# Attention in a fused trunk kernel: probability transposes in groups of two tiles, value products one group behind, across query blocks

## The chip, the core and the metric

The kernel runs on one core of a Trainium2 chip. The metric is the device time of one execution in microseconds. Five engines work from queues of their own, each in order: TensorE (PE for its matrix products, PEld for its weight loads), VectorE (DVE), ScalarE (ACT), GpSimd (POOL) and SyncE (SP), which here issues all DMA transfers.

## The reference, cut to what matters

One layer of a decoder: RMS norm, an input projection, then a diagonal state-space mixer (SSM with a gated unit, GLU) beside a causal attention with forget gates, an output projection, and a squared-ReLU MLP. The part that the change touches is the attention, in float32, with 8 heads of 64 over 2048 positions:

```python
s = einsum('bhqd,bhkd->bhqk', qb, kb) * scale
s = s + csum[:, :, q0:kend, None] - csum[:, :, None, :kend]
s = where(mask, s, -inf)
p = softmax(s, axis=-1)
out = einsum('bhqk,bhkd->bhqd', p, vb)
```

## The kernel before, in words

Full float32 products are made of three (in attention two) products of reduced-precision operands: each operand is split into a rounded part (`h`) and a remainder (`l`).

Attention goes head by head (`h`, 8 of them), and within a head over 8 blocks `b` of 256 queries, each of two rows of 128. For a block, `s_units` makes the scores: for each row and each 512 keys two matmuls into a PSUM bank `s` (L796, L797), of which there are three, then DVE adds the mask and keeps a running minimum (L800), and ACT takes the exponential of the row (L804), into a buffer `p`.

`t_units` then works over `j`, one step for 256 keys. `tr(j)` transposes the four 128x128 tiles of `p` on PE into one PSUM bank `t`, of three (L832; the three tiles on the diagonal in L839 to L841). ACT copies the bank to the rounded part `th` (L853), and DVE makes the remainder `tl` from bank and `th` (L854). `th` and `tl` have THB = 3 buffers each; the diagonal uses `lasth` and `lastl`, two of each. `pv(j)` multiplies `vs` with them: L863 with `th` and L864 with `tl`, twice each, all adding up in the one PSUM bank `o` of the block. A list of steps holds the order: transposes of `j`, then products of `j-1`:

```python
hold[j] = tr(j)
if j:
    pv(j - 1, hold.pop(j - 1))
```

The products of the last `j` close the block, `fin1` copies `o` to `ot` (L868), and `fin2`, put off until after the next block's steps, transposes `ot` back (L874), adds its halves (L877, L878) and stores them to `o_d` (L879).

Between blocks a generator (`side`) issues pieces of the SSM (L587 to L643) and the GLU (L699 to L725), whose matmuls run on the same PE. When the attention's pools are closed, the output projection takes their memory: `woh` and `wol` are made on ACT (L979) and DVE (L980) from loaded weights, and L1019 to L1021 multiply with them. So `woh` waits until the last `oo` is stored.

What is written is not yet the order on the engines. A scheduler places all instructions, engine by engine, by the order in which they are written and by its own estimate of when their operands are ready; so instructions of neighbouring blocks and of the side work stand between the steps above.

Of the kernel before, what the change touches and what calls it, by code (L numbers as in the profile page):

```python
# [37 lines left out]
AHEAD = 1  # L38
LAG = 3
TAB = 2  # L40
THB = 3
SPRI = 150
FGJ = 5
FGC = 3
# [23 lines left out]
def f32(ap):  # L68
    return ap.bitcast(F32)


def body(tc, a, out, stop=None):
# [3 lines left out]
    with ctx:  # L76
# [657 lines left out]
        with ExitStack() as pb:  # L734
# [20 lines left out]
            def load_head(h):  # L755
                r0 = h * HD
                k2 = k2s[h % 2]
                k1 = kv[h % 2].tile([P, L], R, tag="k1", name="k1") if h else AT["k1"]
                vs = (kv1v if h % 2 else kv0).tile([P, NT, P], R, tag="vs", name="vs") if h else AT["vs"]
                nc.sync.dma_start(out=f32(k1[0:HD]), in_=kh_d[r0:r0 + HD])  # L760
                nc.sync.dma_start(out=f32(k1[HD:]), in_=kh_d[r0:r0 + HD])
                nc.sync.dma_start(out=f32(k2[0:HD]), in_=kl_d[r0:r0 + HD])
                nc.sync.dma_start(out=f32(k2[HD:HD + 2]), in_=c_d[h])
                nc.sync.dma_start(out=f32(vs), in_=v_d[h])
                hd[h] = (k1, k2, vs)
# [56 lines left out]
            def t_units(h, b):  # L822
                po = {}

                def tr(j):
                    q0, q1 = pt_[h, 2 * b], pt_[h, 2 * b + 1]
                    pt = ps_t.tile([P, CH], F32, tag="t", name="t")
                    if j < b:
                        k = 0
                        for kt in (2 * j, 2 * j + 1):  # L830
                            for q in (q0, q1):
                                T.transpose(pt[:, k:k + P], q[:, kt * P:(kt + 1) * P], ident)  # L832
                                k += P
                        th = ab.tile([P, CH], R, tag="th", name="th", bufs=THB)
                        tl = ab.tile([P, CH], R, tag="tl", name="tl", bufs=THB)
                        o = 0
                        kts = (2 * j, 2 * j + 1)
                    else:
                        T.transpose(pt[:, 2 * P:3 * P], q0[:, 2 * j * P:(2 * j + 1) * P], ident)  # L839
                        T.transpose(pt[:, 3 * P:4 * P], q1[:, 2 * j * P:(2 * j + 1) * P], ident)  # L840
                        T.transpose(pt[:, P:2 * P], q1[:, (2 * j + 1) * P:(2 * j + 2) * P], ident)  # L841
                        th, tl = lh[nlast[0] % 2], ll[nlast[0] % 2]
                        nlast[0] += 1
                        o = P
                        kts = (2 * j + 1, 2 * j)
                    nt[0] += 1
                    if j < b and nt[0] % POOLT == 0:
                        t = ab.tile([P, CH], F32, tag="tf", name="tf")
                        S.activation(t, pt, AF.Copy)
                        G.tensor_copy(th, t)  # L850
                        G.tensor_tensor(out=tl, in0=t, in1=f32(th), op=ALU.subtract)
                    else:
                        S.activation(th[:, o:], pt[:, o:], AF.Copy)  # L853
                        V.tensor_tensor(out=tl[:, o:], in0=pt[:, o:], in1=f32(th[:, o:]), op=ALU.subtract)  # L854
                    return th, tl, kts

                def pv(j, x):
                    th, tl, kts = x
                    vs = hd[h][2]
                    if j == 0:  # L860
                        po["o"] = ps_o.tile([P, 256], F32, tag="o", name="o")
                    for n, kt in enumerate(kts):
                        T.matmul(po["o"], vs[:, kt, :], th[:, n * 256:n * 256 + 256], start=(j == 0 and n == 0), stop=False)  # L863
                        T.matmul(po["o"], vs[:, kt, :], tl[:, n * 256:n * 256 + 256], start=False, stop=(j == b and n == 1))  # L864

                def fin1():
                    ot = ab.tile([P, 256], F32, tag="ot", name="ot")
                    S.activation(ot, po["o"], AF.Copy)  # L868
                    po["ot"] = ot

                def fin2():
                    pt = ps_t.tile([P, CH], F32, tag="t", name="tt")
                    for n in range(2):
                        T.transpose(pt[:, n * P:(n + 1) * P], po["ot"][:, n * P:(n + 1) * P], ident)  # L874
                    oo = ab.tile([P, 2, HD], F32, tag="oo", name="oo", bufs=3)
                    p3 = pt[:, :256].rearrange("p (n d) -> p n d", d=P)
                    S.activation(oo, p3[:, :, HD:], AF.Copy)  # L877
                    V.tensor_tensor(out=oo, in0=p3[:, :, :HD], in1=oo, op=ALU.add)  # L878
                    nc.sync.dma_start(out=o_d[b * 256:(b + 1) * 256, h * HD:(h + 1) * HD].rearrange("(n p) d -> p n d", p=P), in_=oo)  # L879

                hold = {}
                us = []
                for j in range(b + 1):
                    def u(j=j):
                        hold[j] = tr(j)
                        if j:
                            pv(j - 1, hold.pop(j - 1))
                    us.append(u)

                def end():  # L890
                    pv(b, hold.pop(b))
                    fin1()
                us.append(end)
                return us, fin2

            load_head(0)
            defer = []
            pss = ExitStack()

            def stages():  # L900
# [9 lines left out]
            for h in range(H):  # L910
                for n, b in enumerate(FIRST if h == 0 else range(8)):
                    if n == (2 if h == 0 else 0) and h + 1 < H:
                        load_head(h + 1)
                    with tc.high_priority(offset=SPRI if h == 0 and n < 2 else 0):
                        for u in s_units(h, b):
                            u()
                    tu, fin2 = t_units(h, b)
                    for u in tu:
                        u()
                    if defer:  # L920
                        defer.pop()()
                    defer.append(fin2)
                    marks.append(next(x for x in reversed(nc.cur_bb.bb.instructions) if x.engine == mybir.EngineType.PE))
                    credit += (b + 2) * (RATE2 if wr else RATE)
                    while credit >= 1 and chunks[0] < 1:
                        credit -= 1
                        if len(marks) > LAG:
                            with tc.issue_after(marks[-1 - LAG]):
                                next(side, None)
                        else:  # L930
                            next(side, None)
            defer.pop()()
            while chunks[0] < 1:
                next(side)
# [473 lines left out]
```

## Time and profile before

| | before |
|---|---|
| median of 3 runs | 2467.52 us (2463.4 to 2474.23) |
| profiled execution | 2465.18 us, of which its span 2463.4 us |
| PE busy, share of the span | 2395.5 us, 97% |
| PE weight loads busy | 2012.4 us, 82% |
| DVE busy | 1603.4 us, 65% |
| ACT busy | 1142.8 us, 46% |
| POOL busy | 855.4 us, 35% |
| mean granted TensorE clock | 0.99 |

Attention begins with its first transposes at 407.8 us and its last value product starts at 932.9 us. "Busy" of PE counts each matmul from start to a modelled end, so neighbours overlap: the distance from one start to the next is what a matmul costs. A clock of 1.00 is 2.4 GHz, one of 0.50 is 1.2 GHz. In the groups of rows below, the "idle before" of a group is the time in which its engine did nothing, and the name behind the arrow is what ended it.

### The profile page before, as it was taken

To read this page: it belongs to the slowest core of one execution; us is meant where nothing else is said; L and a number is where in the kernel's file an instruction comes from. 1 tells how busy PE (TensorE), PEld (TensorE's weight loads), DVE (VectorE), ACT (ScalarE), POOL (GpSimd) and SP (SyncE) were. 2 spreads that over 40 slices of the span, in tenths; PEclk is the share of its full clock that TensorE was granted. 3 is DMA by queue.
4 is the path that set the end of the run, shared out by engine and by line. 5 is a ranking of instruction groups with operands and counts; after the bars stand their busy time and mean duration, and the time that the engine had idled before them with its cause. 6 is when DMAs were issued, how large, how long until landed. Compare 5 with 4: busy or idle time off the path is not lost.

```text
span 2463.4 us, 35859 instructions
## 1 busy us (share of the span) xinstructions
PE 2395.5 (97%) x12208; PEld 2012.4 (82%) x12208; DVE 1603.4 (65%) x2996; ACT 1142.8 (46%) x1914; POOL 855.4 (35%) x810
## 2 busy tenths in 40 slices
PE   7999999999999998999899999999999999999998
PEld 6988888899889877888678887788888888788886
DVE  7513424888888798767456657856775565686675
ACT  4312214777667685333344444444544444444343
POOL 2077302445443165322445443320124444332110
PEclk9999999999999999999899999999999999999999
DMA  5455534455454355666444447777764444586774
GB/s 198 133 151 163 170 120 125 112 130 129 118 127 122 75 142 160 212 227 222 143 145 149 143 160 282 246 234 239 252 203 144 137 146 154 209 290 216 247 236 148
DMA packets 286871, 428.49 MB, mean 174 GB/s; under 512 B 80656, under 2 KB 130320, under 8 KB 284112
## 3 DMA queue, kind: packets, MB, share of 16 engines
q1 hardware_dynamic: 286688, 426.21, 54.8%
q8 instruction: 96, 1.57, 0.3%
q14 instruction: 87, 0.71, 0.1%
HBM read 284.93 MB, written 141.16 MB: 173 GB/s over the span
## 4 chain that ended last, share of the span: by engine, by line
PE 56%; DVE 2%; DMA 1%; issue 1%; POOL 1%; ACT 0%; SPq 0%; DVEq 0%; ACTq 0%; POOLq 0%
PE pp L1143 8%; PE pp L1144 8%; PE pp L1145 8%; PE pp L1241 8%; PE pp L1242 8%; PE pp L1240 7%; PE po L1020 2%; PE po L1019 2%; PE po L1021 2%; PE pt L958 1%; DVE y L1106 0%; DVE olo L1233 0%; DVE olo L1099 0%; PE pz L710 0%; PE pz L709 0%
## 5 line engine op out<-in xcount | busy, mean ns | idle before, releaser
L1098 ACT ACTIVATE ohi<-raw 128x1024 fp32r<-128x1024 f32 x224 | 222.9, 999 | 432.8 <-PE pp L1144 199.8
L1099 DVE TENSOR_TENSOR olo<-raw,ohi 128x1024 fp32r<-128x1024 f32 x224 | 283.4, 1277 | 178.6 <-ACT ohi L1098 174.6
L1241 PE MATMUL pp<-olo,ohi 128*128 128x512 f32 x896 | 350.6, 391 | 3.2 <-DVE olo L1233 3.2
L1242 PE MATMUL pp<-ohi,olo 128*128 128x512 f32 x896 | 348.9, 390 | 0.0
L1240 PE MATMUL pp<-ohi 128*128 128x512 f32 x896 | 340.3, 391 | 0.7 <-ACT ohi L1232 0.7
L1143 PE MATMUL pp<-xh_t,ohi 128*128 128x512 f32 x512 | 203.1, 397 | 3.5 <-DVE u L1106 2.5
L1144 PE MATMUL pp<-xl_t,ohi 128*128 128x512 f32 x512 | 202.2, 395 | 0.0
L1145 PE MATMUL pp<-xh_t,olo 128*128 128x512 f32 x512 | 201.9, 395 | 0.0
L1241 PEld LDWEIGHTS pp<-olo,ohi 128*128 128x128 f32 x896 | 168.5, 188 | 39.0 <-DVE olo L1233 4.4
L1240 PEld LDWEIGHTS pp<-ohi 128*128 128x128 f32 x896 | 168.3, 188 | 36.5 <-ACT ohi L1232 1.3
L1242 PEld LDWEIGHTS pp<-ohi,olo 128*128 128x128 f32 x896 | 168.6, 188 | 34.8
L854 DVE TENSOR_TENSOR tl<-t,th 128x512 fp32r<-128x512 f32 x224 | 150.3, 686 | 42.3 <-ACT th L853 41.4
L804 ACT ACTIVATE p<-p,m 128x1920 f32<-128x1920 f32 (+15 forms) x128 | 154.0, 1204 | 28.4 <-DVE m L800 27.9
L1103 POOL TENSOR_TENSOR s<-h,h 128x512 f32<-128x512 f32 x32 | 57.2, 1789 | 300.1 <-DVE olo L1099 224.1
L1143 PE MATMUL pp<-xh_b,ohi 128*128 128x512 f32 x384 | 153.0, 398 | 4.4 <-DVE xl_t L961 2.4
L853 ACT ACTIVATE th<-t 128x512 fp32r<-128x512 f32 x224 | 129.0, 596 | 58.6 <-PE t L832 50.5
L1144 PE MATMUL pp<-xl_b,ohi 128*128 128x512 f32 x384 | 152.3, 397 | 0.2 <-DVE xl_b L961 0.2
L373 PE MATMUL pm<-xl,whi 128*128 128x512 f32 x384 | 152.1, 396 | 0.0
L1145 PE MATMUL pp<-xh_b,olo 128*128 128x512 f32 x384 | 152.0, 396 | 0.0
L374 PE MATMUL pm<-xh,wlo 128*128 128x512 f32 x384 | 151.8, 395 | 0.0
L372 PE MATMUL pm<-xh,whi 128*128 128x512 f32 x384 | 151.8, 396 | 0.0
L796 PE MATMUL s<-k,qs 128*128 128x512 f32 (+2 forms) x320 | 135.1, 424 | 1.5 <-DVE m L800 1.4
(438 smaller groups left out, 5975.0 us busy)
## 6 DMA issues: line engine op xcount, KB each, us to landing
raw<-q_d SPq DMA_DIRECT2D x224, 256.0 KB
raw<-in_w_down SPq DMA_DIRECT2D x224, 256.0 KB
raw<-in_w_up SPq DMA_DIRECT2D x64, 512.0 KB
q_d<-s SPq DMA_DIRECT2D x128, 256.0 KB
q_d<-h SPq DMA_DIRECT2D x96, 256.0 KB
xr<-n_d SPq DMA_DIRECT2D x48, 256.0 KB
x<-in_x SPq DMA_DIRECT2D x16, 512.0 KB
v_d<-sv SPq DMA_DIRECT2D x32, 256.0 KB
```

The costliest lines, as they stand in the source:

```text
L372: T.matmul(ps, hi[:, k, :], xh[c][:, k, :], start=(k == 0), stop=False)
L373: T.matmul(ps, hi[:, k, :], xl[c][:, k, :], start=False, stop=False)
L374: T.matmul(ps, lo[:, k, :], xh[c][:, k, :], start=False, stop=(k == KT - 1))
L804: S.activation(pr[:, :kend], pr[:, :kend], AF.Exp, bias=m[:, ch:ch + 1], scale=-1.0, accum_out=l_all[:, i, h:h + 1])
L1098: S.activation(hi[:, sl], src, AF.Copy)
L1099: V.tensor_tensor(out=lo[:, sl], in0=src, in1=f32(hi[:, sl]), op=ALU.subtract)
L1143: T.matmul(pb, wh[:, ks], XH[xn][:, k], start=start and k == 0, stop=False, skip_group_check=not start)
L1144: T.matmul(pb, wh[:, ks], XL[xn][:, k], start=False, stop=False, skip_group_check=not start)
L1145: T.matmul(pb, wl[:, ks], XH[xn][:, k], start=False, stop=stop and k == 3, skip_group_check=not start)
L1240: T.matmul(banks[i], hi[:, 0, isl], hi[:, 1], start=start and u == 0, stop=False, **sk)
L1241: T.matmul(banks[i], hi[:, 0, isl], lo[:, 1], start=False, stop=False, **sk)
L1242: T.matmul(banks[i], lo[:, 0, isl], hi[:, 1], start=False, stop=u == 15, **sk)
```

## The change: what it does

`t_units` no longer returns steps. It walks over `j` in groups of GRP = 2. For each group it first issues a `fin2` that is still put off, then the transposes of both tiles of the group (eight of them, or fewer on the diagonal), and then the value products of the group ahead of it, which lie in a list `waiting`. That list is kept across query blocks and heads: the last group of a block is multiplied only after the first group of the next block is transposed. `fin1` follows the last products of a block. `th` and `tl` get six buffers each instead of three. What an engine computes is the same, and so is the number of instructions on each engine.

```diff
-THB = 3
+THB = 6
+GRP = 2
...
-                hold = {}
-                us = []
-                for j in range(b + 1):
-                    def u(j=j):
-                        hold[j] = tr(j)
-                        if j:
-                            pv(j - 1, hold.pop(j - 1))
-                    us.append(u)
-
-                def end():
-                    pv(b, hold.pop(b))
-                    fin1()
-                us.append(end)
-                return us, fin2
+                def pvs(g):
+                    def f():
+                        for j, x in g:
+                            pv(j, x)
+                        if g[-1][0] == b:
+                            fin1()
+                            defer.append(fin2)
+                    return f
+
+                for j0 in range(0, b + 1, GRP):
+                    if defer:
+                        defer.pop()()
+                    g = [(j, tr(j)) for j in range(j0, min(j0 + GRP, b + 1))]
+                    if waiting:
+                        waiting.pop()()
+                    waiting.append(pvs(g))
...
-                    tu, fin2 = t_units(h, b)
-                    for u in tu:
-                        u()
-                    if defer:
-                        defer.pop()()
-                    defer.append(fin2)
+                    t_units(h, b)
...
+            waiting.pop()()
             defer.pop()()
```

The scheduler makes of this another order on every engine, from the first value product on. Two places of it follow. Lines of the changed kernel stand one higher in the attention (L833 for L832, L864 and L865 for L863 and L864, L875 for L874) and one lower in the output projection (L978 for L979).

The first place is on PE, in the seventh head, where a block ends and a long one begins. `t`, `th` and `tl` belong to the tiles of the new block, `lasth` and `lastl` to the diagonal of the old one. Before:

```order
L863 MATMUL o<-lasth_3761,vs 128x256
L832 MATMUL t<-ident,p 128x128 x4
L864 MATMUL o<-lastl_3763,vs 128x256
L863 MATMUL o<-lasth_3761,vs 128x256
L864 MATMUL o<-lastl_3763,vs 128x256
L832 MATMUL t<-ident,p 128x128 x8
L863 MATMUL o<-th,vs 128x256
L864 MATMUL o<-tl,vs 128x256
```

And now:

```order
L864 MATMUL o<-lasth_3761,vs 128x256
L643 MATMUL py<-abz,cs 128x256
L797 MATMUL s<-k_9382,qs 128x512
L798 MATMUL s<-k_1_3756,q_3_3459 128x512
L797 MATMUL s<-k_9382,qs 128x256
L798 MATMUL s<-k_1_3756,q_3_3459 128x256
L865 MATMUL o<-lastl_3763,vs 128x256
L864 MATMUL o<-lasth_3761,vs 128x256
L865 MATMUL o<-lastl_3763,vs 128x256
L875 MATMUL tt<-ident,ot 128x128 x2
L833 MATMUL t<-ident,p 128x128 x8
L864 MATMUL o<-th,vs 128x256
```

Before, the first `th` and `tl` of the new block come from the four transposes five rows above the products. Now those four stand ten rows further up than the piece shown, ahead of three products of the old block, four more transposes and five SSM products.

The second place is at the end of the attention. On ACT, `oo` is the last output of the attention, `woh` the first weights of the output projection, `pq` and `jk` belong to the norm of the GLU's output, and `w` and `gh` to its next chunk. Before:

```order
L877 ACTIVATE oo<-tt 128x128
L979 ACTIVATE woh_11287<-raw,gn 128x1024
L979 ACTIVATE woh_11293<-raw,gn 128x1024
L979 ACTIVATE woh_11299<-raw,gn 128x1024
L979 ACTIVATE woh_11305<-raw,gn 128x1024
```

And now:

```order
L878 ACTIVATE oo<-tt 128x128
L688 ACTIVATE w<-w 128x512 x2
L726 ACTIVATE jk,ss_s<-pq 128x512
L700 ACTIVATE gh<-gt 128x512 x2
L726 ACTIVATE jk,ss_s<-pq 128x512 x3
L978 ACTIVATE woh_11287<-raw,gn 128x1024
L978 ACTIVATE woh_11293<-raw,gn 128x1024
```

The four `jk` and their neighbours, which stood behind the first weights, now stand ahead of them. On PE the sixteen transposes that make `pq` go with them, directly behind the last two of the attention:

```order
L712 MATMUL pz<-gh,wl 128x512
L875 MATMUL tt<-ident,ot 128x128 x2
L724 MATMUL pq<-ident,sg 128x128 x16
L710 MATMUL pz<-gh,wh 128x512
L711 MATMUL pz<-gl,wh 128x512
L712 MATMUL pz<-gh,wl 128x512
```

Before, there were gate products (`pz`) there, and the transposes for `pq` came between products of the output projection.

## Rows read from the trace of the kernel before

**Rows 1.** Busy time by stage: us, PE, PEld, DVE, ACT, POOL, clock, DMA share, GB/s
```profile
407.00:934.00 527.00, 516.01 (x3536) 464.71 (x3534) 442.68 (x1095) 382.87 (x749) 233.56 (x250) 1.00 0.48 120
934.00:956.00 22.00, 15.52 (x57) 11.38 (x58) 19.06 (x26) 13.53 (x17) 11.08 (x9) 0.84 0.46 145
```

**Rows 2.** Waits of weight loads, 407 to 934 us: total us, times, longest
```profile
PEld o L864 <- DVE tl L854: 8.9, 24, 1.3
PEld s L796 <- DVE m L800: 5.1, 14, 0.7
...
PEld o L863 <- ACT ot L868: 2.5, 7, 0.6
...
PEld o L863 <- ACT th L853: 1.1, 4, 0.4
...
PEld o L864 <- DVE lastl L854: 0.4, 2, 0.2
```

**Rows 3.** Timeline around 848 us: start us, us, instruction [idle before, what ended it]
```profile
847.59 0.60 PE L832 MATMUL t<-ident,p 128*128 128x128 f32 x4
...
848.28 0.60 ACT L853 ACTIVATE th<-t 128x512 fp32r<-128x512 f32 x1 [0.38 <-PE t L832]
848.38 1.04 PE L832 MATMUL t<-ident,p 128*128 128x128 f32 x8
...
848.91 2.06 DVE L854 TENSOR_TENSOR tl<-t,th 128x512 fp32r<-128x512 f32 x3 [3.60 <-ACT th L853]
...
849.66 0.19 PEld L864 LDWEIGHTS o<-tl,vs 128*128 128x128 f32 x1 [0.26 <-DVE tl L854]
```

**Rows 4.** Timeline around 855 us, where DVE waited for a load
```profile
855.37 0.17 DVE L669 TENSOR_SCALAR gb<-gb 128x4 f32<-128x4 f32 x1 [1.46 <-DMA gb<-in_glu_b]
855.44 0.68 DVE L854 TENSOR_TENSOR tl<-t,th 128x512 fp32r<-128x512 f32 x1
...
856.18 0.19 PEld L864 LDWEIGHTS o<-tl,vs 128*128 128x128 f32 x1 [1.30 <-DVE tl L854]
```

**Rows 5.** Groups by line: xcount, busy us, mean ns, idle before, its releaser
```profile
L832 PE MATMUL t<-ident,p 128*128 128x128 f32 x896 | 130.7, 272 | 0.0
```

**Rows 6.** Timeline of PE alone around 659 us
```profile
658.60 0.60 PE L832 MATMUL t<-ident,p 128*128 128x128 f32 x4
658.95 0.36 PE L863 MATMUL o<-th,vs 128*128 128x256 f32 x1
659.15 0.28 PE L864 MATMUL o<-tl,vs 128*128 128x256 f32 x1
659.27 0.28 PE L863 MATMUL o<-th,vs 128*128 128x256 f32 x1
```

**Rows 7.** Busy time by stage at the end of attention, columns as above
```profile
932.00:938.00 6.00, 3.75 (x22) 3.09 (x21) 5.90 (x12) 2.33 (x4) 3.85 (x3) 1.00 0.50 142
938.00:944.00 6.00, 4.03 (x19) 2.81 (x18) 4.10 (x7) 1.10 (x3) 5.52 (x5) 1.00 0.05 11
944.00:950.00 6.00, 2.90 (x7) 1.62 (x8) 5.06 (x4) 6.00 (x7) 3.64 (x3) 0.76 0.29 98
950.00:956.00 6.00, 6.00 (x22) 4.73 (x21) 6.00 (x9) 5.17 (x7) 0.00 (x0) 0.67 0.88 286
```

**Rows 8.** Timeline of ACT, 939 to 961 us
```profile
939.08 0.27 ACT L877 ACTIVATE oo<-tt 128x128 f32<-128x128 f32 x1
943.75 4.27 ACT L979 ACTIVATE woh<-raw,gn 128x1024 fp32r<-128x1024 f32 x4 [4.41 <-DMA o_d<-oo]
...
950.52 1.14 ACT L687 ACTIVATE w<-w 128x512 f32<-128x512 f32 x2
...
955.63 0.57 ACT L725 ACTIVATE jk<-pq 128x512 f32<-128x512 f32 x1
956.11 0.19 ACT L725 ACTIVATION_READ_ACCUMULATOR jk<-pq 128x1 f32 x1
956.20 2.19 ACT L699 ACTIVATE gh<-gt 128x512 fp32r<-128x512 f32 x2
```

More of the change, by code (lines that the diff above doesn't have):

```diff
@@ L879, in fin2 @@
                     nc.sync.dma_start(out=o_d[b * 256:(b + 1) * 256, h * HD:(h + 1) * HD].rearrange("(n p) d -> p n d", p=P), in_=oo)
-                hold = {}
-                us = []
-                for j in range(b + 1):
-                    def u(j=j):
-                        hold[j] = tr(j)
-                        if j:
-                            pv(j - 1, hold.pop(j - 1))
-                    us.append(u)
-                def end():
-                    pv(b, hold.pop(b))
-                    fin1()
-                us.append(end)
-                return us, fin2
+                def pvs(g):
[13 more added lines that the diff above has]
+                    waiting.append(pvs(g))
             load_head(0)
-            defer = []
+            defer, waiting = [], []
             pss = ExitStack()
```

## The prediction, made before the result was known

> **What bounds the kernel now.** I read the busy time by stage first, then the waits, then the timeline at the places where they stand. By stage, the attention with its side work, from 407 to 934 us, is a stretch in which PE is busy 516 of 527 us at a clock of 1.00 [rows 1]. DVE is busy for 443 us of it and ACT for 383: neither is the bound, but DVE has little room. So a change of order can win only what PE loses in there, and PE's busy time hides some of that, since each matmul is counted to a modelled end. The waits of the weight loads show more of it [rows 2]: 8.9 us for `tl`, 0.4 for `lastl` and 1.1 for `th`, together 10.4 us in 30 waits, that is for the operands of the value products; 5.1 us for a free score bank (DVE must have read it); 2.5 us for the single bank `o`, which ACT must have emptied before the next block's first product. That is 18.0 us, or 0.7% of the time, and it is about all that the middle of the kernel can give.
>
> How such a wait comes about is seen at 848 us [rows 3]. The four transposes of a block's first tile start at 847.59 at 0.11 us apart ((1.04 - 0.27) / 7 in the eight at 848.38, 0.27 being the length of one [rows 5]), so their slot is over at 848.03. `th` starts at 848.28 and takes 0.60, the first `tl` starts at 848.91, and the weight load with it at 849.66, 1.63 us after the slot. In that time PE had three products at 0.12, eight transposes at 0.11 and one more product, 1.36 us of work. The missing 0.27 us is the wait of 0.26 that the row shows. So an undisturbed tile needs about 1.6 us of other work on PE between its transposes and its `tl`, and one more DVE instruction of 0.6 us in the way makes it 2.2 us. At 855 us it was worse: DVE sat behind a load for 1.46 us, and PE waited 1.30 us for the `tl` behind it [rows 4].
>
> At the end of attention stands the other loss: from 932 to 950 us PE is busy for 3.75, 4.03 and 2.90 of three times 6 us, idle for 7.3, and the clock then stands at 0.76 and 0.67 in two stretches [rows 7]. The chain there is the last `oo`, its store, then `woh`, since the new weights take the attention's memory: ACT idles 4.41 us until the store is done [rows 8].
>
> **The change, part by part.** No instruction is added or removed, so all of it is distance and order.
>
> *Operands of the value products.* I counted in both orders, with 0.11 us for a transpose, 0.12 for a value product, 0.23 for a score product of 512 and 0.22 for an SSM product, the PE work between the last transpose of a tile and the first product with its `tl`. Over the 288 tiles the smallest distance goes from 1.23 to 1.70 us, the median from 3.18 to 3.53, and the tiles with less than 2.2 us go from 64 to 27. At the first place shown with the change it goes from 1.36 to about 4.5 us. In proportion to those tiles, 27/64 of the 10.4 us stay, 4.4 us, and 6.0 go. But waits like that at 855 us come from DVE being held up and depend on the distance less; so I take 5.5 us of gain. The ends are 0 (all waits are of that kind) and 10.4 us.
>
> *Score banks.* There are three, and a bank is used again three score tiles later. Counted in the same way, from the end of the products of one use to the start of those of the next but two, distances under 2.0 us go from 19 to 31 of 317. In proportion the 5.1 us become 8.3, 3.2 more; most reuses are far from that limit, and the tiles in question lie only just under it, so I take a loss of 1.0 us. Ends: a gain of 5.1 (DVE, less often pressed, frees them earlier) and a loss of 3.2.
>
> *The bank `o`.* Distances under 1 us from a block's last product to the next block's first go from 13 to 10 of 63. I count nothing; the ends are a gain of 2.5 and a loss of 1.0, since ACT's queue between the two is another one now.
>
> *Alternation of transposes and products.* From transposing (or another full-precision product) to a product PE changes 346 times before and 314 times after. At 658.60 four transposes and the product behind them take 0.55 us to the start of the next but one matmul [rows 6], and 4 x 0.11 + 0.12 is 0.56: the product starts early and the one behind it later by as much. So an alternation costs nothing, and neither do 32 of them. If the 0.08 us by which the first product's slot is longer than 0.12 were all a price, it would be 2.6 us, which is the end on the gaining side.
>
> *Transpose banks.* Eight transposes need two of the three banks `t` at once. No transpose waited before (0.0 [rows 5]); the shortest twentieth of the reuse distances goes from 2.17 to 1.93 us, still over 1.6. I count nothing, with a loss of 2 us as the end, about what the `th` waits and half of the `o` waits are now. The six `th` and `tl` buffers only take away waits of ACT, which is not the bound.
>
> *The end of attention.* The sixteen transposes for `pq` now stand ahead of the output projection: 16 x 0.11 = 1.8 us of work moves into idle time. Against that, ACT no longer waits idle for the last store; it has two `w` (1.14 us), four `jk` (0.57 + 0.19 each) and two `gh` (2.19) to do between `oo` and `woh` [rows 8], 6.4 us against the 4.41 of before, so `woh` may come 2.0 us later, which is 0.2 us more than the moved work covers. The last value products themselves may be earlier, since their `lastl` has more time. I take a gain of 1.5 us; the ends are a gain of 5 (two thirds of the 7.3 us idle filled) and a loss of 6 (below).
>
> The sum: -5.5 + 1.0 + 0 + 0 + 0 - 1.5 = -6.0 us. The profiled execution took 2465.18 us, 1.8 of it outside its span; it becomes 2459 us. The median of the runs lies 2.3 us above that execution, and a rise of that size is within their own spread.
>
> **A rule that speaks against it.** In the stage of attention, with nearly 1100 transposes (896 of them in L832 [rows 5]), the clock is granted at 1.00 throughout [rows 1], the eight in a row at 848.38 included [rows 3]. The Trainium skill, in "TensorE: Matmul & The Clock Gate", Part 4 on PE-mode transpose, says that the full clock does not engage for transposes, as they don't count as PE activity in the same way. By that rule longer runs of transposes would invite falls of the clock; the trace does not agree so far, as its runs of eight did not lose it.
>
> **Rivals.**
>
> *All of the middle's waits go* (18%). All 18.0 us of rows 2 vanish and the end gives its 1.5: 2465.2 - 19.5 = 2446 us. For it: each of these waits is short (1.3 us at the longest), and the smallest distance now exceeds 1.6 us. Against it: score banks come closer together, and DVE is busy for 84% of the stage.
>
> *It does not do what it says* (24%). The scheduler fills gaps by itself and pulls the groups apart again: runs of eight transposes go from 20 to 22 only, and runs of four from 167 to 161. DVE's queue has the same work, so a product that comes later finds a `tl` that comes later, and waits move to the score banks: 2466 us, no change. For it: the median distance grew by only 0.35 us, and DVE's hold-ups [rows 4] stay.
>
> *The end of attention gets slower* (12%). The four `pq` go through one bank, so each needs its four transposes (0.44 us) and its `jk` (0.76), with the two `gh` between: 4 x 1.20 + 2.19 = 7.0 us before `woh` can start, 2.6 more than the 4.41 us. PE then idles long enough for one more fall of the clock, which cost 0.24 x 6 + 0.33 x 6 = 3.4 us of full clock in rows 7. With nothing won in the middle that is 2465.2 + 6.0 = 2471 us, slower than before. It decides if `woh` starts more than 7.3 us after `oo`, that is 2.6 more than the 4.67 between 939.08 and 943.75 [rows 8]. Against it: some of the `jk` work stood in PE's way later anyway.
>
> *The clock falls in attention* (3%). One fall like that at 950 us costs 0.33 x 6 = 2.0 us; one for each of 8 heads makes 16 us and 2481 us. Rows 1 speak against it.
>
> **How the numbers follow.** The forecast above has 43%, with a range of its own from 2453 to 2465 us. Half a per cent of 2467.5 is 12.3 us, about what a measurement of this kernel can tell from no change. Faster than 2455.2: the first rival, 18%, and 10 of the 43: 28%. Slower than 2479.9: 4 of the 12% of the slower end, if it also costs a later fall, and the 3% of the clock: 7%. The remaining 65% are no change. For 8 in 10 I go from the first rival to a little above the slower end: 2446 to 2473 us.
>
> **What the changed profile would show.** Right: waits for `tl`, `lastl` and `th` under 6 us in the attention's stage, those for score banks at 5 to 8, the value products' last start 3 to 6 us earlier, the idle time from there to the first product of the output projection below 7 us, and a clock of 1.00 throughout the attention. Wrong in the sizes: waits of 9 us or more on `tl` (then closeness was not their cause), transposes that wait for a bank, or `woh` more than 7 us behind `oo`. Wrong as a whole: the attention's end moved by more than 15 us, for then PE was losing time there that no wait in the rows shows.

## The result, and the profile after

The changed kernel takes 2483.93 us at the median (2480.49 to 2485.4) against 2467.03 us of the kernel before: a ratio of 1.0065, 95% interval 1.0048 to 1.0081. It is slower by some 16 us, where 6 us less had been forecast. Its profiled span is 2479.4 us (before 2463.4), its mean clock 0.99 as before. Busy times hardly differ: PE 2393.0 us (2.5 less), DVE 1607.1 (3.7 more), ACT 1144.9 (2.1 more). So the 16 us are waiting on PE.

Lines of the attention now carry numbers higher by one (L833 transposes into `t`, L864 and L865 value products, L854 and L855 `th` and `tl`, L869 `ot`, L875 `tt`, L878 and L879 `oo`), those of the output projection numbers lower by one (L978 `woh`). First the busy time by stage, with the columns of [rows 1]:

```profile
407.00:934.00 527.00, 505.86 (x3487) 453.76 (x3486) 434.45 (x1078) 377.40 (x738) 223.50 (x245) 1.00 0.48 120
946.00:952.00 6.00, 4.79 (x26) 3.51 (x23) 5.19 (x9) 3.28 (x5) 5.21 (x4) 1.00 0.01 3
952.00:958.00 6.00, 0.26 (x1) 0.26 (x2) 4.02 (x5) 2.77 (x7) 4.20 (x3) 0.55 0.99 251
958.00:964.00 6.00, 3.09 (x12) 1.89 (x11) 2.01 (x2) 3.47 (x8) 1.04 (x1) 0.50 0.62 110
964.00:970.00 6.00, 5.84 (x15) 4.60 (x16) 5.72 (x8) 4.89 (x7) 5.57 (x5) 0.53 0.17 58
```

In the same 527 us PE is busy for 10.2 us less than in [rows 1], and 49 fewer matmuls get through. Behind the attention, whose last value product has moved from 932.9 to 946.5 us, PE idles 10.0 of 24 us (946 to 970), and the clock is at its lower level (0.50) or near it for 18 us; before, [rows 7] has two stretches of 6 us below 1.00, at 0.76 and 0.67. So there are two places to look at: the attention itself and its end.

**In the attention.** The waits of PE's weight loads, now up to the attention's new end at 947 us, beside [rows 2]:

```profile
PEld tt L875 <- ACT ot L869: 13.6, 19, 1.9
PEld s L797 <- DVE m L801: 8.0, 17, 1.0
...
PEld o L865 <- DVE tl L855: 4.3, 8, 1.2
...
PEld t L833 <- DVE oo L879: 0.8, 1, 0.8
PEld t L833 <- DVE tl L855: 0.7, 2, 0.4
...
PEld o L864 <- ACT th L854: 0.5, 2, 0.2
```

The waits that the prediction priced go the way it said or stay within its ends: `tl`, `lastl` and `th` together fall from 10.4 to 4.8 us, the score banks rise from 5.1 to 8.0, the 2.5 us for the bank `o` are gone, and transposes wait 1.5 us for a bank `t` (no such row before). On top stands a row that the list of before does not have: 13.6 us in which the transposes of `fin2`, `tt`, wait for `ot`. The sum of these rows is 27.9 us, against 18.0 in [rows 2].

How such a wait comes about, from the timeline of the changed kernel (PE, ACT and DVE, around 444 us):

```profile
441.58 0.28 PE L865 MATMUL o<-lastl,vs 128*128 128x256 f32 x1
...
441.63 1.14 ACT L805 ACTIVATE p<-p,m 128x1024 f32<-128x1024 f32 x1
...
442.11 0.34 PE L798 MATMUL s<-k,q 128*128 128x384 f32 x1
...
442.76 0.81 ACT L805 ACTIVATE p<-p,m 128x640 f32<-128x640 f32 x1
...
443.57 0.37 ACT L869 ACTIVATE ot<-o 128x256 f32<-128x256 f32 x1
...
443.99 0.44 PE L875 MATMUL tt<-ident,ot 128*128 128x128 f32 x2 [1.55 <-ACT ot L869]
...
444.26 1.04 PE L833 MATMUL t<-ident,p 128*128 128x128 f32 x8
...
444.78 0.29 DVE L879 TENSOR_TENSOR oo<-tt,oo 128x128 f32<-128x128 f32 x1 [1.92 <-ACT oo L878]
```

The block's last product starts at 441.58. Between it and `tt` PE has only the four score matmuls, until 442.4. ACT meanwhile is at the exponentials of two rows, 1.14 and 0.81 us, and comes to `ot` at 443.57, 1.7 us after the bank is complete. So PE stands for 1.55 us, and behind `tt` in its queue are the next group's eight transposes, which need nothing from `ot`. DVE waits as well, 1.92 us, since `oo` of this block is the next in its queue. That ACT took `ot` only after the exponentials ahead of it agrees with the Trainium skill, "PSUM — Partial Sum Buffer", section "Engine vs sequencer instructions", by which the queues of ScalarE, VectorE and GpSimd are strictly first in, first out.

Not every one of the 19 waits is of this kind. In 11 of them, 9.6 us together, ACT has exponentials or a `th` to finish when the bank is complete. In the other eight, 4.0 us, it is idle and takes `ot` at once, and PE waits all the same, since it has next to nothing between the last product and `tt`, here nothing:

```profile
524.87 0.38 ACT L869 ACTIVATE ot<-o 128x256 f32<-128x256 f32 x1 [0.17 <-PE o L865]
525.30 0.20 PEld L875 LDWEIGHTS tt<-ident,ot 128*128 128x128 f32 x2 [0.68 <-ACT ot L869]
```

**At the end of the attention.** ACT in the changed kernel, beside [rows 8]:

```profile
952.28 0.25 ACT L878 ACTIVATE oo<-tt 128x128 f32<-128x128 f32 x1
955.17 0.63 ACT L688 ACTIVATE w<-w 128x512 f32<-128x512 f32 x1 [2.63 <-POOL w L687]
956.39 0.63 ACT L688 ACTIVATE w<-w 128x512 f32<-128x512 f32 x1 [0.59 <-POOL w L687]
957.00 0.60 ACT L726 ACTIVATE jk<-pq 128x512 f32<-128x512 f32 x1
...
957.59 2.04 ACT L700 ACTIVATE gh<-gt 128x512 fp32r<-128x512 f32 x2
...
964.01 4.25 ACT L978 ACTIVATE woh<-raw,gn 128x1024 fp32r<-128x1024 f32 x4
```

and PE in the same stretch:

```profile
951.56 0.33 PE L724 MATMUL pq<-ident,sg 128*128 128x128 f32 x1 [0.54 <-DVE sg L718]
957.74 1.12 PE L724 MATMUL pq<-ident,sg 128*128 128x128 f32 x4 [5.85 <-ACT jk L726]
960.26 1.12 PE L724 MATMUL pq<-ident,sg 128*128 128x128 f32 x4 [1.40 <-ACT jk L726]
962.21 1.11 PE L724 MATMUL pq<-ident,sg 128*128 128x128 f32 x4 [0.84 <-ACT jk L726]
964.16 0.80 PE L710 MATMUL pz<-gh,wh 128*128 128x512 f32 x1 [0.84 <-ACT jk L726]
```

`woh` starts 11.7 us after `oo`, not 4.7 as in [rows 8]. The first `jk`, which empties the one bank of `pq`, stands in ACT's queue behind two `w` that POOL has not finished: 2.63 and 0.59 us of waiting. So the second four of `pq` wait 5.85 us and the others 1.40 and 0.84, and everything behind them on PE, the output projection too, comes later: its first product at 969.5 us (before 945.0). Of these 24.5 us 13.6 are there at the last value product, and 10.9 come between the two. Not all of it is loss. Work has moved ahead: 16 more matmuls than before stand ahead of the last value product (12 `pz`, 4 `pt`) and 28 more ahead of that first product (12 `pz`, 16 `pq`). And the time at the lower clock, which lay mostly behind it in [rows 7], now lies ahead of it. From there to its end the changed kernel takes 1510.0 us, 8.4 less than before.

### The profile page after: what moved, and what is told of

It is laid out like the page before. It is cut to its first block, busy times and chain, and to the rows that moved or that the text cites. A ratio compares the mean times of both kernels' runs of the same rounds, so it can differ in the third digit from the quotient of the medians.

```text
span 2479.4 us, 35864 instructions
## 1 busy us (share of the span) xinstructions
PE 2393.0 (97%) x12208; PEld 2007.9 (81%) x12208; DVE 1607.1 (65%) x2996; ACT 1144.9 (46%) x1914; POOL 854.7 (34%) x810
## 4 chain that ended last, share of the span: by engine, by line
PE 79%; DVE 7%; POOL 5%; issue 3%; DMA 3%; ACT 2%; SPq 0%; DVEq 0%; ACTq 0%; POOLq 0%
PE pp L1142 8%; PE pp L1143 8%; PE pp L1144 8%; PE pp L1240 8%; PE pp L1241 7%; PE pp L1239 7%; PE t L833 3%; PE po L1018 2%; PE po L1020 2%; PE po L1019 2%; PE pm L374 2%; PE pm L373 2%; PE pm L375 2%; PE s L797 2%; PE o L865 2%
## 5 line engine op out<-in xcount | busy, mean ns | idle before, releaser
L855 DVE TENSOR_TENSOR tl<-t,th 128x512 fp32r<-128x512 f32 x224 | 149.1, 684 | 28.3 <-ACT th L854 27.7
L854 ACT ACTIVATE th<-t 128x512 fp32r<-128x512 f32 x224 | 129.3, 595 | 46.7 <-PE t L833 46.3
L797 PE MATMUL s<-k,qs 128*128 128x512 f32 (+2 forms) x320 | 128.6, 403 | 3.7 <-DVE m L801 3.6
```

The source lines that it names most:

```text
L797: T.matmul(ps[:, o:o + w], q1[:, qsl], k1[:, c0 + o:c0 + o + w], start=True, stop=False)
```

## The experiments

Two things differ from what was priced: where `fin2` stands, and the order at the end. Seven kernels tell them apart, each timed against the kernel before on the same chip.

**fin2 later.** The changed kernel, with `fin2` behind the products that follow the next block's first group (its old place was behind all of the next block's steps).

```diff
-                    if defer:
-                        defer.pop()()
+                    old = defer[:]
+                    del defer[:]
                     g = [(j, tr(j)) for j in range(j0, min(j0 + GRP, b + 1))]
                     if waiting:
                         waiting.pop()()
+                    for f in old:
+                        f()
```

> The changed kernel, with the last transposes of a block (fin2) issued after the next group's value products instead of right before that group's transposes. Theory A: the changed kernel's loss has two places: fin2 stands right behind fin1 on PE, so PE waits for ACT's copy ot (13.6 us of weight loads waiting in the attention), and the end of attention, where sixteen transposes for pq stand in a row ahead of the output projection. Here fin2 has at least 0.9 us of other PE work behind the last product, so the waits on ot fall below 2 us; the sixteen pq transposes don't stand in a row any more in its order either, so the end is cheaper too: 2457 to 2466 us. Rival B: grouping and crossing blocks cost by themselves (score banks, DVE's queue): waits on ot go, others come, 2478 us or more.

Measured: 2461.67 us (2457.52 to 2464.1), ratio 0.9972 (0.9961 to 0.9982). This one move takes back all 16 us and 6 more. The waits of its weight loads, 407 to 934 us:

```profile
PEld s L797 <- DVE m L801: 3.1, 6, 1.5
...
PEld o L865 <- DVE tl L855: 1.7, 7, 0.3
PEld t L833 <- DVE tl L855: 1.5, 4, 0.5
PEld o L864 <- ACT ot L869: 1.4, 3, 0.6
```

The wait of `tt` is gone from the list and the products' waits for `tl` stay small, so the groups do what they were forecast to do. The score banks, too, are back below 5.1 us, so their rise to 8.0 came with the early `fin2` and not with the groups. Transposes now wait for a bank `t`, 1.5 us in the row above. The row of `pq` at the end is gone with it: `woh` starts at 934.52 us, 7.2 after its `oo` at 927.36, and the output projection at 935.7 us. So this run alone can't say which of the two places costs how much; it does say that the groups, which it keeps in all eight heads, cost nothing on balance.

**The last head in the old order.** The changed kernel, with head 7 alone issued as before (single tiles, one product behind, `fin2` after them).

```diff
+                if h == H - 1:
+                    prev = None
+                    for j in range(b + 1):
+                        x = tr(j)
...
+                        if prev is not None:
+                            pv(*prev)
+                        prev = (j, x)
+                    pv(*prev)
+                    fin1()
...
+                    return
```

> The changed kernel, but in the last of the 8 heads the transposes, products and fin2 are issued as before the change. Theory A: the end of attention has its old order, which gives back what the last head and the end cost (5.6 and 7.7 us more lost on PE than before), the waits on ot in the other heads stay at 11 to 13 us: 2469 to 2474 us. Rival B (grouping as such costs): 7/8 of the loss stays, 2480 us or more. Rival C (all of the loss is at the end): 2467 us or less, with no wait on ot that matters.

Measured: 2468.04 us (2464.83 to 2471.36), ratio 1.0000 (0.9992 to 1.0009).

```profile
PEld tt L875 <- ACT ot L869: 13.3, 18, 1.9
```

Theory A's range began at 2469 us, 1 us above. In heads 0 to 6 the waits for `tt` are all still there (13.3 of the 13.6 us), and yet the kernel is no slower than the one before: there they cancel against what the groups win. Nearly the whole net loss lies in the last head and at its end. `oo` and `woh` stand at 938.41 and 944.18 us, 5.8 us apart.

**Both undone.** `fin2` late in heads 0 to 6, and the last head as in the run above.

```diff
+                    old = defer[:]
+                    del defer[:]
...
+                    for f in old:
+                        f()
```

> Late fin2 in the first seven heads and the last head as before the change. Theory A: both losses gone, the gain on tl and lastl stays: 2457 to 2462 us, waits on ot under 2 us, waits on tl, lastl and th under 7 us, end of attention within 3 us of the kernel before. Rival B: 2475 us or more.

Measured: 2459.61 us (2458.33 to 2468.12), ratio 0.9971 (0.9960 to 0.9982): the fastest of all, though not to be told from the first run.

```profile
PEld o L865 <- DVE tl L855: 4.5, 12, 1.3
...
PEld o L864 <- ACT ot L869: 1.7, 4, 0.6
```

Against the run before it, in which only `fin2` of heads 0 to 6 stands elsewhere, it gains 0.29% or 7 us. That is the price of the early `fin2` in those heads, about half of its 13.3 us of waits. And against the kernel before it gains 7 us: that is what groups and crossing in seven heads, with six buffers, are worth without the two mishaps.

**Six buffers only.** The kernel before, with THB = 6.

```diff
-THB = 3
+THB = 6
```

> The kernel before with six th and tl buffers instead of three, nothing else. Theory A: the buffers alone do nothing: 2464 to 2470 us, waits on tl as before (8 to 10 us). A rival by which the buffers themselves slow the kernel (memory placed elsewhere, other waits) would show 2475 us or more.

Measured: 2464.92 us (2461.63 to 2470.75), ratio 0.9987 (0.9978 to 0.9997), 1 to 5 us faster.

```profile
PEld o L864 <- DVE tl L854: 9.3, 26, 1.3
PEld s L796 <- DVE m L800: 5.1, 13, 0.7
```

The waits of PE in the attention are those of [rows 2], so the buffers alone change nothing there. Nor does the attention end earlier: of the 2.6 us between the spans of the two profiled executions (2460.8 and 2463.4), 0.3 are there at the last product of the output projection (1167.1 and 1167.4 us), and the rest lies behind it, in the MLP, which the edit doesn't touch. In the profiles of all nine kernels that last part takes 1293.8 to 1296.7 us. A gain by the buffers is not shown.

**Only the last block in the old order.** As the last-head run, for block 7 of head 7 alone.

```diff
-                if h == H - 1:
+                if h == H - 1 and b >= 7:
```

> The changed kernel, but the last block of the last head alone is issued as before (single tiles, one product behind; its fin2 where it was). That flips the end of the order: woh stands again ahead of the jk of the four pq, while heads 0 to 6 and seven blocks of head 7 stay as changed. Theory A (the net loss is the end: ACT's jk, which stand behind two w that wait for POOL, hold woh and the output projection back): woh starts 4.4 to 7 us behind oo, the first product of the output projection comes at 942 to 950 us and not at 969.5, the waits of tt for ot stay at 12 to 15 us, and the time is 2466 to 2471 us. Rival B (the last head loses its time over all of its blocks and the row of pq is only where that shows): the last value product stays at 943 to 948 us, and the time is 2476 to 2482 us.

Measured: 2474.36 us (2472.49 to 2479.48), ratio 1.0023 (1.0014 to 1.0032), between the two theories. ACT at the end:

```profile
948.32 0.28 ACT L878 ACTIVATE oo<-tt 128x128 f32<-128x128 f32 x1
953.59 4.27 ACT L993 ACTIVATE woh<-raw,gn 128x1024 fp32r<-128x1024 f32 x4 [5.00 <-DMA o_d<-oo]
```

`woh` follows `oo` after 5.3 us, as theory A said, and the time from the last value product to the first of the output projection is 10.2 us (944.6 to 954.8) instead of 22.9 (946.5 to 969.5); the kernel before has 12.1 (932.9 to 945.0). The waits of `tt` are the same 13.6 us. So the order of the last block, with the row of `pq` ahead of `woh`, costs 0.42%, 10 us, which is the larger part. But the last value product, at 944.6 us, stays where rival B had it, and here B is right: the other blocks of head 7 lose something too, 0.23% or 6 us against the last-head run. The weight loads' wait for score banks from 858 to 948 us is one part of it:

```profile
PEld s L797 <- DVE m L801: 5.0, 7, 1.8
```

In the last-head run it is 1.5 us (858 to 936). In this run's profile the clock fell inside head 7:

```profile
898.00:904.00 6.00, 5.38 (x22) 4.98 (x23) 5.21 (x12) 1.98 (x5) 3.71 (x4) 0.50 0.06 14
```

The changed kernel has no such fall there. What it cost can be read off, since PE has the same order in both kernels for the first 5525 matmuls, up to 928.1 us of the changed one, and each matmul can be set beside itself. In this run they come 3.0 us later than in the changed kernel ahead of the fall (893 us), 5.7 later behind it (899 us), and 3.8 later at 928.1 us, for later waits have taken up most of it. So the fall cost 2.7 us at first and under 1 us in the end. The 3.0 us were there from earlier, some 1.5 of them from another fall of the clock, between 419 and 431 us (0.85 and 0.86 in two stretches of 6 us), and say how far two executions of one order can lie apart. From the last matmul of the common order to its end the changed kernel takes 9.8 us more than this one, which agrees with the 10 us above.

**Early fin2 alone.** The kernel before, with one edit: a `fin2` that is put off is issued ahead of the next block's steps.

```diff
                     tu, fin2 = t_units(h, b)
-                    for u in tu:
-                        u()
                     if defer:
                         defer.pop()()
+                    for u in tu:
+                        u()
                     defer.append(fin2)
```

> The kernel before, with one edit: a put-off fin2 is issued ahead of the next block's transposes and not behind them. In its order 43 of 63 tt come under 1 us of work behind the last product (1 before, 22 in the changed kernel), and 174 tiles have under 2.2 us between transposes and tl (64 before, 27 in the changed kernel). Theory A (a tt close behind the last product waits for ot, in proportion to the close ones, at 13.6 us for 22; a tl close behind its transposes waits likewise, at 10.4 us for 64): waits of tt for ot of 20 to 27 us and of tl of 20 to 28 us in the attention, and a time of 2495 to 2515 us. Rival B (the waits come from the groups and not from the place of fin2): tt waits under 5 us, and 2466 to 2475 us.

Measured: 2554.8 us (2551.43 to 2556.92), ratio 1.0349 (1.0329 to 1.0368), 85 us slower. Its waits up to the attention's end at 1038 us:

```profile
PEld s L796 <- DVE m L800: 27.9, 75, 0.8
PEld o L864 <- DVE tl L854: 27.1, 68, 1.9
PEld tt L874 <- ACT ot L868: 15.3, 23, 1.2
PEld o L864 <- DVE lastl L854: 9.9, 43, 2.2
PEld t L832 <- DVE oo L878: 9.2, 6, 3.7
PEld o L863 <- ACT th L853: 8.5, 14, 2.3
```

The waits that theory A named are there, but the size was far off. `tl` is within its range (27.1 of 20 to 28), `tt` below it (15.3 of 20 to 27), and three kinds were not counted: score banks, `lastl` and `th`, and transposes that wait for the early `oo` to give their bank back. The six rows sum to 97.9 us, 79.9 more than [rows 2], which is nearly all of the 85. An early `fin2` costs more than its own wait: the scheduler places all else anew around it, and the work between transposes and `tl` shrinks, as the counts in the expectation say. So the groups of the changed kernel seem to have covered most of what its early `fin2` would have cost.

**Groups of one tile.** The changed kernel with GRP = 1 and `fin2` late as in the first run.

```diff
-GRP = 2
+GRP = 1
```

> The changed kernel with groups of one tile (four transposes), across blocks as there, and fin2 issued behind the products that follow the next block's first tile. Its order has 67 tiles under 2.2 us (64 before, 27 in the changed kernel), 34 score banks under 2.0 us (19 and 31), 21 tt under 1 us, none under 0.44, and at the end twelve pq in a row whose jk stand ahead of woh, as in the changed kernel. Theory A (close tl and the row of pq ahead of woh cost time): tl waits of 8 to 11 us, tt waits of 4 to 8 us, woh 8 us or more behind oo, first product of the output projection at 952 us or later, and 2474 to 2484 us. Rival B (the row of pq is no cost by itself, and groups of eight are what loses): 2462 to 2470 us, first product of the output projection before 948 us.

Measured: 2483.3 us (2483.2 to 2488.87), ratio 1.0064 (1.0047 to 1.0081), as theory A had it in time. Waits from 407 to 934 us, and ACT at the end:

```profile
PEld o L864 <- ACT ot L869: 10.6, 18, 1.2
PEld o L865 <- DVE tl L855: 10.1, 31, 1.2
```

```profile
955.75 0.63 ACT L688 ACTIVATE w<-w 128x512 f32<-128x512 f32 x1 [3.45 <-POOL w L687]
...
960.57 0.28 ACT L878 ACTIVATE oo<-tt 128x128 f32<-128x128 f32 x1
...
966.26 1.14 ACT L980 ACTIVATE woh<-raw,gn 128x1024 fp32r<-128x1024 f32 x1
```

`tl` is back at 10.1 us, near [rows 2], for 67 close tiles against 64: it is the groups of eight, not the crossing of blocks, that take this wait away. `ot` is waited for 10.6 us, in the next block's first product, which with single tiles comes too soon behind the block's last. The waits of `tt` for it, expected at 4 to 8 us, do not show up from 407 to 934 us; one of 4.38 us comes at the end, where `ot` stands on ACT behind a `w` that waits for POOL and two `gh`. At the end the detail was wrong too: `woh` is only 5.7 us behind `oo`, because here four `pq` stand ahead of `tt` and `oo` itself is late. From the last value product (953.3) to the first of the output projection (971.6) it is 18.3 us all the same, with ACT behind a `w` for 3.45 of them.

## Why the prediction was wrong, point by point

**The step that failed** is one that is not in it: the part "The change, part by part" prices five effects in the attention and one at its end, but not the move of `fin2` itself. That the change issues it first stood in the description, and its two transposes came out right behind the last products in the order shown there. Counted in the same way as the prediction's other distances, the work on PE between a block's last product and `tt` falls from a median of 4.40 to 1.31 us, and 22 of 64 `tt` have less than 1 us (before: one). For `tl` the prediction asked how much work PE has between the transposes and the product that needs their result; for `tt`, which needs `ot` from ACT, it asked neither that nor what ACT has ahead of `ot` (1.95 us of exponentials in the rows above). Put at nothing, the early `fin2` showed 13.6 us of waits, and moving it alone takes back all of the loss. A second term had the wrong sign: the end of attention stood in the sum as a gain of 1.5 us, and it cost some 10.

**Terms that held.** *Operands of the value products*: 5.5 of 10.4 us gained by forecast, 5.6 measured (10.4 to 4.8). *Score banks*: by proportion 8.3 us, and I took only a third of the rise; it is 8.0, so the choice was 2 us too low for this kernel. But the cause was another than the groups, for with `fin2` late it is 3.1. *The bank `o`*: nothing by forecast, 2.5 us gained, its end. *Transpose banks*: nothing by forecast with 2 us as the end, 1.5 us measured. *Alternation* was nothing by forecast, and no run sets it apart. *The sum* of the middle's terms without `fin2` was about 4.5 us, and the sum with the end 6; with `fin2` later the runs gain some 7. That these agree is in part luck: the score banks, put at a loss of 1.0, gain 2.0 us in the first of these runs.

**The clock in the attention** of the changed kernel stayed at 1.00 throughout, with runs of eight transposes. The rule from the Trainium skill ("TensorE: Matmul & The Clock Gate", Part 4), that the full clock does not engage for transposes, does not agree with this trace either, in which they stand among products; the rival built on it (3%) is out. Where the clock fell in head 7 of another run, it did so behind a wait, not in a row of transposes.

**The end of attention** as a loss was a rival with 12%, and its mechanism came: `woh` 11.7 us behind `oo`, over the 7.3 that decide it. Its size was too small, 6.0 us where some 10 were measured. It summed only busy time (four `pq` with `jk`, two `gh`); the two `w` are not in it, and in the sum of the forecast itself they stand at 1.14 us of work, not at the 3.2 us that they wait for POOL. And it was set beside a middle with nothing won, not beside a new wait.

**How the 16 us are made up**, by ratios to the kernel before (each step 0.1 to 0.2% uncertain): groups and crossing in heads 0 to 6, with six buffers, -0.29%; early `fin2` in heads 0 to 6 +0.29%; the new order in blocks 0 to 6 of head 7, groups and early `fin2` together, +0.23%; the last block's order, with the row of `pq` at the end, +0.42%. Together +0.65%, as it must be, for each step is the difference between one run and the next. The steps are not independent causes: with `fin2` later in all heads, the last three go together. Of the signs that were to show the forecast right, the waits (4.8 us, under 6; 8.0, within 5 to 8) and the clock came as written; that the last value product would come 3 to 6 us earlier (it came 13.6 later), and less than 7 us of idle time behind it, did not. Of the signs against it in its sizes two came: transposes that wait for a bank, and `woh` more than 7 us behind `oo`. What stays open: why the new order costs 6 us in seven blocks of head 7 and on balance nothing in the seven heads before. In the waits, 3.5 us of the 6 are score banks (5.0 against 1.5); the rest was not found.

## What to carry to other kernels

When a change moves a small step along with a large one, follow the small one's operands to the engine that makes them, and read from the timeline what that engine has ahead of it. Here a wait on PE held up all that stood behind it, and later waits took back only a part; so put work that needs another engine's answer behind work that does not, even where that engine is idle. And in a kernel ordered by a scheduler, a move in one place can change the order far away, here at the end of the attention: look there for a bank that is emptied behind something that is late itself.

## What the runs showed of the hardware that was not expected

The same order with the same waits does not always keep the clock. At nearly the same place PE has the same products and the same wait in the changed kernel and in the run with only the last block in the old order. For some 30 us before, each matmul of the second run comes 3.0 to 3.1 us after its like in the first. In the first the granted clock is 1.00 from 892 to 904 us, and the next gate product starts after 0.35 us:

```profile
895.60 0.51 PE L711 MATMUL pz<-gl,wh 128*128 128x512 f32 x1 [1.80 <-DVE gl L701]
895.95 0.39 PE L712 MATMUL pz<-gh,wl 128*128 128x512 f32 x1
```

In the second the clock is 0.50 from 898 to 904 us, and the next starts after 0.60 us:

```profile
898.62 0.79 PE L711 MATMUL pz<-gl,wh 128*128 128x512 f32 x1 [1.79 <-DVE gl L701]
899.22 0.63 PE L712 MATMUL pz<-gh,wl 128*128 128x512 f32 x1
```

No row told the two apart ahead of the fall.
